# The third group of dilated query and key tiles as four plain tiles, with fewer weight sums and another pace for the rest

## The chip, the core and the metric

The kernel runs on one core of one Trainium2 chip. The metric is the device time of one execution in microseconds, the median over runs. The core has a matrix engine (TensorE, PE in the profile, with its weight loads as PEld), VectorE (DVE), ScalarE (ACT) and GpSimd (POOL); SyncE (SP) issues most of the loads, POOL issues other DMAs, and 16 DMA engines move the data of both queues.

## The reference

One decoder layer over x of 512 tokens x 1024 channels, in float32. A single projection of x gives queries, keys and values of three causal token mixers and three gates:

```python
proj = x @ w_in
(da_q, da_k, da_v, sb_q, sb_k, sb_v, dl_q, dl_k, dl_v, gates) = jnp.split(proj, _split_points(), axis=-1)
...
merged = (g[:, :, 0] * (o_da @ w_branch_da) + g[:, :, 1] * (o_sb @ w_branch_sb)
          + g[:, :, 2] * (o_dl @ w_branch_dil))
return merged @ w_out
```

`da` is differential attention (4 heads), `sb` stick-breaking attention (8 heads), `dl` dilated attention: three window groups of 4 heads of 128 channels, so `dl_q` and `dl_k` have 12 column tiles of 128 each. Output head `hd` of the dilated mixer needs the tiles `4 * g + hd` of the three groups g. After the mixer come a layer norm, a squared-ReLU MLP with 4096 hidden channels, a gated per-layer embedding and a second layer norm:

```python
x = layer_norm(DEEPNORM_ALPHA * x + m, ln1_g[i], ln1_b[i])
hid = jax.nn.relu(x @ w_up[i])
c = jnp.square(hid) @ w_down[i]
ple = jax.nn.sigmoid(x @ w_ple_gate[i]) * (p[i] @ w_ple[i])
x = layer_norm(DEEPNORM_ALPHA * x + c + ple, ln2_g[i], ln2_b[i])
```

## The kernel before

**Precision.** Every large product is done with both operands split into a high and a low part, as three matmuls: high x high, high x low, low x high (`mm3`, L86 to L89). Weights come from DRAM in chunks of 128 x 1024 (512 KB) into a ring of six raw buffers; ACT casts a chunk to its high part (L262), DVE subtracts to get the low part (L264), into a ring of five pairs. `pump` and `split_next` run these splits ahead of TensorE. SP issues the loads (`fill`, L194 to L219) in the order of the chunks, one queue in order: a load that must wait for its data or for a free buffer holds up all loads behind it.

**Items.** The work of TensorE is a list of items in a fixed order (`main_order`, L36 to L53, then the gates, branches, output projection, embedding and MLP). The loop at L2177 walks through it. Around each item it calls `step()`, which lets the attention heads that are in flight (Python generators: `sb_head`, `da_block`, `dil_head`) emit their next piece; an item whose `mm` is a generator with one `yield` gets a second `step()` in its middle. So attention is woven between the projection's matmuls.

**A plain tile** ("T", `t_item`, L311) is one item: one weight chunk, eight k blocks, three matmuls of 512 columns each, 24 in all, and its result is put away by one operation over 512 columns (L343 on ACT for `dl_q`, L346 on DVE for `dl_k`).

**A group** ("G", `group_items`, L354) computes four tiles, that is two query-key pairs, with seven products in place of eight: weights and x are cut into 2 x 2 blocks, and sums of weight blocks meet sums of x blocks. Each product is taken for both pairs over half of the tokens (256 columns): 7 x 2 x 4 x 3 = 168 matmuls, in seven items. It uses seven weight chunks, three from the weights themselves and four that are sums of weight blocks (`qsum`), and puts its results away in halves (L394, L396, L398, L407, L440 and L441). There are three groups, each of which holds two query-key pairs of the dilated heads 2 and 3. Groups 0 and 1 lie behind the value tiles; group 2 lies between the second and the third differential query-key pair, and dilated head 3 needs it.

**Weight sums.** The same scheme of seven products serves values, gates, branches and the MLP. All their weight sums are made in DRAM by DMAs that POOL issues (`sum_steps`, L1212): a plain copy of a 512 KB block to a scratch tensor or an accumulating copy onto it. A sum of the kind `up_steps` takes eight steps, of the kind `two_steps` four, of `down_steps` eight; the queue of them is in the order of use (values, `qsum`, gates `msum` and branches `bsum`, `gsum`, then the MLP's `usum` and `dsum`), with four sums in progress at a time, and two towards its end. Each step of a sum waits on POOL's queue until the step before it in that sum has landed. The loads of `usum` and `dsum` chunks by SP wait for the sum in turn. POOL's queue also carries the dilated heads' value stores and loads (`keep` L520, `values_of` L528) and the accumulations straight into a raw buffer (`then_add`, L176).

**Pace.** When a step is emitted is set by credits (L2222 to L2228): each item adds its `size` times its `rate`, and each whole credit emits one step. Items without a rate of their own get 2.8, 2.3 or 3.3 by their place in the list (L960); those with 3.3 are the differential query and key tiles. Group items have 0.6 (L382), output projection items 1.4 (L1055), of which those before `wout_at + 6` count. From the last of the embedding's items on, each item adds 0.78 (L2225). There are 208 steps in all. On POOL each step also waits for a mark, a recent operation of DVE, so that steps do not run far ahead of the stream.

Of the kernel before, what the change touches and what calls it, by code (L numbers as in the profile page):

```python
# [10 lines left out]
F32 = mybir.dt.float32  # L11
# [7 lines left out]
P = 128  # L19
# [16 lines left out]
def main_order():  # L36


    o = [("T", "sb_q", 0), ("T", "sb_k", 0), ("T", "sb_q", 1), ("T", "sb_k", 1), ("V", "sb_v", 0)]
    for j in (2, 3):  # L40
        o += [("T", "sb_q", j), ("T", "sb_k", j)]
    for h in range(2):
        for g in range(3):
            o += [("T", "dl_q", 4 * g + h), ("T", "dl_k", 4 * g + h)]
    o += [("V", "dl_v", 0), ("V", "da_v", 0), ("V", "dl_v", 1), ("V", "dl_v", 2)]
    pairs = [(("dl_q", 4 * g + h), ("dl_k", 4 * g + h)) for h in (2, 3) for g in range(3)]
    groups = [("G", tuple(pairs[2 * i:2 * i + 2]), i) for i in range(3)]
    o += groups[:2]
    for d in range(4):
        if d == 2:  # L50
            o += groups[2:]
        o += [("T", "da_q", d), ("T", "da_k", d)]
    return o  # L53


def trunk(tc, a, out):
    nc = tc.nc
    es = ExitStack()
    with es:
# [4 lines left out]
        dram = es.enter_context(tc.tile_pool(name="dram", bufs=1, space=bass.MemoryType.DRAM))  # L64
# [9 lines left out]
        def slot(name, dt=F32):  # L74
            return big.tile([P, 512], dt, name=nm(name), tag="s", bufs=NSLOT)

        def small(name, n):
            return one.tile([P, n], F32, name=nm(name), tag=f"sm{n}", bufs=12 if n < 8 else 8)
# [89 lines left out]
        def chunk(src, w):  # L168
            return chunk_of(load(src, w))
# [114 lines left out]
        items = []  # L284
# [21 lines left out]
        T = {}  # L306
# [42 lines left out]

        HB = slice(0, 256)  # L350
        HC = slice(256, 512)
        qsum = [[dram.tile([P, 1024], F32, name=f"qsum{m}_{i}") for i in range(4)] for m in range(3)]

        def group_items(gi, pairs):  # L354

# [601 lines left out]
            item([], mm, ev, size=0.08)  # L957

        for j, it in enumerate(items):
            it.setdefault("rate", 2.8 if j < 12 else 2.3 if j < 52 else 3.3)  # L960

        gate_alone(0, 1)
        gate_alone(1, 2)
# [64 lines left out]
        def wout_items():  # L1028
            for half in range(2):
                cs = [chunk(a["wo"][half, c].rearrange("p k n -> p (k n)"), 1024) for c in range(4)]  # L1030
                for tt in range(4):
                    ks = (4, 5, 6, 7, 0, 1, 2, 3) if tt == 2 and not half else range(8)

                    def mm(ps, tt=tt, cs=cs, ks=ks):
                        for k in ks:
                            c = cs[k // 2]
                            s = slice((k % 2) * 512, (k % 2) * 512 + 512)
                            h, lo = merged_T[k // 4, tt // 2, k % 4 // 2]
                            q = slice(k % 2 * 256 + tt % 2 * P, k % 2 * 256 + tt % 2 * P + P)
                            nc.tensor.matmul(ps, h[:, q], c["h"][:, s], start=k == ks[0], stop=False)  # L1040
                            nc.tensor.matmul(ps, h[:, q], c["l"][:, s], start=False, stop=False)
                            nc.tensor.matmul(ps, lo[:, q], c["h"][:, s], start=False, stop=k == ks[-1])  # L1042

                    def ev(ps, tt=tt, half=half):
                        y = xn.pop((tt, half))
                        if not half:
                            x1sum[tt] = small("lsm", 2)
                        i = nc.vector.scalar_tensor_tensor(y, y, ALPHA, ps, op0=OP.mult, op1=OP.add,
                                                           accum_out=x1sum[tt][:, half:half + 1])
                        st["added"] = getattr(i, "ins", i)  # L1050
                        x1[tt, half] = y
                        if half:
                            pending.append(ln1_gen(tt))
                    item(cs if tt == 3 else [], mm, ev, need=cs, bank=at_bank)
                    items[-1]["rate"] = 1.4  # L1055
                    for t in {0: [(1, 1, 0), (1, 1, 1)], 1: [(0, 1, 0), (0, 1, 1)]}.get(tt, ()) if not half else ():
                        turn_item(*t)

# [153 lines left out]
        def sum_steps():  # L1212
            def up_steps(sums, w, flat=False):
                w = [w[i] if flat else w[i].rearrange("p k n -> p (k n)") for i in range(4)]
                a1, a2, a3, a4 = sums
                yield a1, w[2], False
                yield a3, w[0], False
                yield a1, w[3], True
                yield a3, w[2], True
                yield a2, a1, False  # L1220
                yield a2, w[0], True
                yield a4, a2, False
                yield a4, w[1], True

            def two_steps(sums, w, flat=False):
                w = [w[i] if flat else w[i].rearrange("p k n -> p (k n)") for i in range(4)]
                a1, a2 = sums
                yield a1, w[2], False
                yield a1, w[3], True
                yield a2, a1, False  # L1230
                yield a2, w[0], True

            def down_steps(m):
                w = [a["wd"][m, i].rearrange("p k n -> p (k n)") for i in range(4)]
                b1, b2, b3, b4 = dsum[m]
                yield b1, w[0], False
                yield b3, w[1], False
                yield b1, w[1], True
                yield b3, w[3], True
                yield b2, b1, False  # L1240
                yield b2, w[3], True
                yield b4, b2, False
                yield b4, w[2], True

            def issue(o, i, plus):
                if plus:
                    i = nc.gpsimd.dma_start(o, i, accum_op=OP.add, max_dma_last_dim=4096)  # L1247
                else:
                    i = nc.gpsimd.dma_start(o, i, max_dma_last_dim=4096)

                tc.add_manual_dep(getattr(i, "ins", i), marks[0].name, mybir.DependencyInfo(
                    mybir.DependencyClass.Sync, mybir.DependencyReason.DATA), reason="spread over the main stream")

            w = a["wv"].rearrange("g c p k n -> g c p (k n)")
            todo = deque(two_steps(vsum[n][m], [w[1 + 2 * n + i // 2, i % 2 * 2 + m] for i in range(4)], True)
                         for n in range(2) for m in range(2))
            todo.extend(up_steps(qsum[m], a["wq"][m]) for m in range(3))
            for n in range(3):
                todo.extend(two_steps(msum[n][m], a["wgm"][n, m]) for m in range(2))
                if n:  # L1260
                    todo.append(up_steps(bsum[2 * (n == 1)], a["wbq"][int(n == 1)]))
            todo.extend(two_steps(gsum[m], a["wg"][m]) for m in range(2))
            for kind, m in ("u0", "u1", "d0", "u2", "u3", "d1", "d2", "u4", "u5", "d3", "d4", "u6", "u7", "d5", "d6"):
                m = int(m)
                todo.append(up_steps(usum[m], a["wu"][m]) if kind == "u" else down_steps(m))
            run = []
            while todo or run:
                while todo and len(run) < (4 if len(todo) > 9 else 2):
                    run.append(todo.popleft())
                for g in list(run):  # L1270
                    s = next(g, None)
                    if s is None:
                        run.remove(g)
                    else:
                        issue(*s)
                        yield
# [338 lines left out]
        wout_at = len(items)  # L1615
# [362 lines left out]
        def dil_head(hd):  # L1978
# [35 lines left out]
            for c in range(4):  # L2014
                s = slice(c * P, c * P + P)
                for g in range(2):
                    o = L12[c // 2][:, (c % 2) * 256 + g * P:(c % 2) * 256 + g * P + P]
# [6 lines left out]
            for c in range(4):  # L2024
                o = L12[c // 2][:, (c % 2) * 256:(c % 2) * 256 + 256]
# [34 lines left out]
            with tc.high_priority():  # L2060
# [3 lines left out]
                for c in range(4):  # L2064
                    o = L12[c // 2][:, (c % 2) * 256:(c % 2) * 256 + 256]
# [5 lines left out]
            if hd == 0:  # L2071
                yield
                values = values_of(hd)
            for _ in range({0: 6, 1: 2, 3: 1}.get(hd, 0)):
                yield

            src0 = {}
# [4 lines left out]
            for half in range(2):  # L2082
# [4 lines left out]
                t = slot("pt0")  # L2087
# [5 lines left out]
            for g in range(2):  # L2093
# [4 lines left out]
                t = slot("pt12")  # L2098
# [5 lines left out]
            for kb in range(4):  # L2104
                n = 256 if kb < 3 else P
# [67 lines left out]
        credit = 0.0  # L2173
# [3 lines left out]
        for n, it in enumerate(items):  # L2177
# [20 lines left out]
            if prev is not None:  # L2198
                prev[0]["ev"](prev[1])
                todo, lead = prev[0].get("then", ((), 0))  # L2200
# [18 lines left out]
            if n == 13:  # L2219
                pending.append(tables())  # L2220

            if 5 <= n < wout_at + 6:  # L2222
                credit += it["size"] * it.get("rate", 1.0)
            elif n > ple_at + 6:
                credit += 0.78  # L2225
            while credit >= 1:
                credit -= 1
                next(sum_steps_, None)  # L2228
# [148 lines left out]
```

## Time and profile before

| | us |
|---|---|
| median of 3 runs | 1032.52 |
| lowest and highest run | 1031.86, 1037.55 |
| the profiled execution | 1029.26 |
| its span, first to last instruction | 1027.5 |

A line of the profile's table of groups names the source line, the engine, the operation, what it writes and reads, the shape, the count, then the busy time, the mean duration of one in ns, and the idle time before it with what ended it. A timeline line gives start, duration, engine, line, operation, tiles, shape and count, and in brackets the idle time before it and what released it. Matmuls are pipelined: a matmul's own duration is longer than the distance to the next one's start, and the distance is what a matmul costs. TensorE's granted clock was 0.999 of full speed in the profiled execution.

### The profile page before, as it was taken

To read this page: it belongs to the slowest core of one execution; us is meant where nothing else is said; L and a number is where in the kernel's file an instruction comes from. 1 tells how busy PE (TensorE), PEld (TensorE's weight loads), DVE (VectorE), ACT (ScalarE), POOL (GpSimd) and SP (SyncE) were. 2 spreads that over 40 slices of the span, in tenths; PEclk is the share of its full clock that TensorE was granted. 3 is DMA by queue.
4 is the path that set the end of the run, shared out by engine and by line. 5 is a ranking of instruction groups with operands and counts; after the bars stand their busy time and mean duration, and the time that the engine had idled before them with its cause. 6 is when DMAs were issued, how large, how long until landed. Compare 5 with 4: busy or idle time off the path is not lost.

```text
span 1027.5 us, 15644 instructions
## 1 busy us (share of the span) xinstructions
PE 1014.6 (99%) x5626; PEld 879.0 (86%) x5626; DVE 794.4 (77%) x1411; ACT 614.7 (60%) x1055; POOL 208.8 (20%) x311
## 2 busy tenths in 40 slices
PE   9999999999999999999999999999999999999997
PEld 6888887888998898888888888889999999999786
DVE  6888697788657776886788885897778778768785
ACT  7566566775544656566655733866666656556551
POOL 0232320121412123111121130222121211111101
PEclk9999999999999999999999999999999999999999
DMA  8999993888999999879999893799999999998932
GB/s 312 286 306 288 259 271 96 209 206 259 288 319 283 253 287 276 220 201 263 352 291 273 294 323 109 182 248 355 338 323 332 318 324 350 327 332 263 297 148 82
DMA packets 79885, 275.99 MB, mean 269 GB/s; under 512 B 9816, under 2 KB 10600, under 8 KB 79808
## 3 DMA queue, kind: packets, MB, share of 16 engines
q0 software_dynamic: 37712, 135.08, 52.4%
q1 hardware_dynamic: 41520, 138.99, 36.6%
q8 instruction: 44, 0.72, 0.3%
q10 hardware_dynamic: 576, 0.92, 0.2%
q14 instruction: 33, 0.27, 0.1%
HBM read 267.59 MB, written 116.42 MB: 374 GB/s over the span
## 4 chain that ended last, share of the span: by engine, by line
PE 92%; DVE 4%; DMA 1%; ACT 1%; issue 1%; DVEq 0%; SPq 0%; ACTq 0%
PE mm L87 9%; PE mm L88 9%; PE mm L89 9%; PE at L1431 4%; PE at L1430 4%; PE at L1432 4%; PE at L752 2%; PE at L751 2%; PE at L750 2%; PE mm L750 2%; PE mm L751 2%; PE mm L752 2%; PE at L89 2%; PE at L88 2%; PE at L87 2%; PE at L1042 1%
## 5 line engine op out<-in xcount | busy, mean ns | idle before, releaser
L264 DVE TENSOR_TENSOR wl<-raw,wh 128x1024 fp32r<-128x1024 f32 (+1 forms) x274 | 330.2, 1214 | 111.4 <-ACT wh L262 110.2
L262 ACT CAST wh<-raw 128x1024 fp32r<-128x1024 f32 (+1 forms) x274 | 283.7, 1042 | 206.9 <-PE mm L88 104.3
L87 PE MATMUL mm<-xhT,wh 128*128 128x512 f32 (+1 forms) x254 | 95.5, 376 | 1.1 <-DVE dl_k L346 1.1
L89 PE MATMUL mm<-xhT,wl 128*128 128x512 f32 (+1 forms) x254 | 94.4, 371 | 0.0
L88 PE MATMUL mm<-xlT,wh 128*128 128x512 f32 (+1 forms) x254 | 94.1, 370 | 0.0
L1431 PE MATMUL at<-wl,hh 128*128 128x512 f32 x188 | 73.8, 393 | 1.0 <-DVE wl L264 1.0
L1430 PE MATMUL at<-wh,hh 128*128 128x512 f32 x188 | 73.9, 393 | 0.5 <-ACT hid L1402 0.5
L1432 PE MATMUL at<-wh,hl 128*128 128x512 f32 x188 | 73.2, 389 | 0.0
L87 PE MATMUL mm<-x1hT,wh 128*128 128x256 f32 x256 | 72.8, 284 | 0.0
L88 PE MATMUL mm<-x1lT,wh 128*128 128x256 f32 x256 | 72.4, 283 | 0.0
L89 PE MATMUL mm<-x1hT,wl 128*128 128x256 f32 x256 | 72.4, 283 | 0.0
L87 PEld LDWEIGHTS mm<-xhT,wh 128*128 128x128 f32 x254 | 47.9, 189 | 8.9 <-issue 1.2
L89 PEld LDWEIGHTS mm<-xhT,wl 128*128 128x128 f32 x254 | 47.8, 188 | 8.3
L88 PEld LDWEIGHTS mm<-xlT,wh 128*128 128x128 f32 x254 | 47.9, 189 | 7.5
L1247 POOL DMA_DIRECT2D usum<-in_wu_dram x32 | 27.0, 843 | 134.5 <-DVE wl L264 61.5
L87 PEld LDWEIGHTS mm<-x1hT,wh 128*128 128x128 f32 x256 | 48.9, 191 | 1.9
L88 PEld LDWEIGHTS mm<-x1lT,wh 128*128 128x128 f32 x256 | 48.9, 191 | 1.5
L89 PEld LDWEIGHTS mm<-x1hT,wl 128*128 128x128 f32 x256 | 48.9, 191 | 0.0
L1247 POOL DMA_DIRECT2D dsum<-in_wd_dram x28 | 24.1, 860 | 106.4 <-DVE wl L264 30.1
L1432 PEld LDWEIGHTS at<-wh,hl 128*128 128x128 f32 x188 | 35.3, 188 | 7.6
L1430 PEld LDWEIGHTS at<-wh,hh 128*128 128x128 f32 x188 | 35.5, 189 | 7.1 <-ACT hid L1402 0.7
L1431 PEld LDWEIGHTS at<-wl,hh 128*128 128x128 f32 x188 | 35.5, 189 | 7.0 <-DVE wl L264 1.3
(676 smaller groups left out, 2857.3 us busy)
## 6 DMA issues: line engine op xcount, KB each, us to landing
usum<-in_wu_dram POOLq DMA_DIRECT2D x48, 512.0 KB, 8.9
dsum<-in_wd_dram POOLq DMA_DIRECT2D x42, 512.0 KB, 8.9
raw<-usum SPq DMA_DIRECT2D x32, 512.0 KB, 8.5
raw<-dsum SPq DMA_DIRECT2D x28, 512.0 KB, 7.8
raw<-in_wt_dram SPq DMA_DIRECT2D x26, 512.0 KB, 7.8
raw<-in_wd_dram SPq DMA_DIRECT2D x25, 512.0 KB, 9.7
raw<-in_wu_dram SPq DMA_DIRECT2D x24, 512.0 KB, 8.3
qsum<-in_wq_dram POOLq DMA_DIRECT2D x18, 512.0 KB, 8.9
```

The lines of the kernel that those rows point to most:

```text
L87: nc.tensor.matmul(ps, wh, xh, start=start, stop=False, skip_group_check=True)
L88: nc.tensor.matmul(ps, wh, xl, start=False, stop=False, skip_group_check=True)
L89: nc.tensor.matmul(ps, wl, xh, start=False, stop=stop, skip_group_check=True)
L262: i = nc.scalar.copy(h, raw)
L264: i = nc.vector.tensor_sub(lo, raw, h.bitcast(F32))
L750: nc.tensor.matmul(ps, h[:, q], c["h"][:, n], start=go, stop=False, skip_group_check=True)
L751: nc.tensor.matmul(ps, h[:, q], c["l"][:, n], start=False, stop=False, skip_group_check=True)
L752: nc.tensor.matmul(ps, lo[:, q], c["h"][:, n], start=False, stop=end, skip_group_check=True)
L1247: i = nc.gpsimd.dma_start(o, i, accum_op=OP.add, max_dma_last_dim=4096)
L1430: nc.tensor.matmul(ps, h[:, q], c["h"][:, s], start=go, stop=False, skip_group_check=True)
L1431: nc.tensor.matmul(ps, h[:, q], c["l"][:, s], start=False, stop=False, skip_group_check=True)
L1432: nc.tensor.matmul(ps, lo[:, q], c["h"][:, s], start=False, stop=end, skip_group_check=True)
```

## The change

Group 2 becomes four plain tiles at the same place, `dl_q` and `dl_k` of its two query-key pairs. Its weight sums (`qsum[2]`, eight steps) are no longer made, so 200 steps are left, and the weights of the group are laid out as plain tiles by the host's `_layout`, which follows `main_order`. The four new tiles take the default rate of their place in the list. That rate goes from 3.3 to 3.0, the output projection's from 1.4 to 2.4 with one item fewer counted, and the MLP's from 0.78 to 0.66. Dilated head 3 waits for one more call of its generator before its weights are transposed (L2074).

```diff
     pairs = [(("dl_q", 4 * g + h), ("dl_k", 4 * g + h)) for h in (2, 3) for g in range(3)]
-    groups = [("G", tuple(pairs[2 * i:2 * i + 2]), i) for i in range(3)]
-    o += groups[:2]
+    o += [("G", tuple(pairs[2 * i:2 * i + 2]), i) for i in range(2)]
     for d in range(4):
         if d == 2:
-            o += groups[2:]
+            o += [("T", *t) for p in pairs[4:] for t in p]
         o += [("T", "da_q", d), ("T", "da_k", d)]
...
-        qsum = [[dram.tile([P, 1024], F32, name=f"qsum{m}_{i}") for i in range(4)] for m in range(3)]
+        qsum = [[dram.tile([P, 1024], F32, name=f"qsum{m}_{i}") for i in range(4)] for m in range(2)]
...
-            it.setdefault("rate", 2.8 if j < 12 else 2.3 if j < 52 else 3.3)
+            it.setdefault("rate", 2.8 if j < 12 else 2.3 if j < 52 else 3.0)
...
-                    items[-1]["rate"] = 1.4
+                    items[-1]["rate"] = 2.4
...
-            todo.extend(up_steps(qsum[m], a["wq"][m]) for m in range(3))
+            todo.extend(up_steps(qsum[m], a["wq"][m]) for m in range(2))
...
-            for _ in range({0: 6, 1: 2, 3: 1}.get(hd, 0)):
+            for _ in range({0: 6, 1: 2, 3: 2}.get(hd, 0)):
                 yield
...
-            if 5 <= n < wout_at + 6:
+            if 5 <= n < wout_at + 5:
                 credit += it["size"] * it.get("rate", 1.0)
             elif n > ple_at + 6:
-                credit += 0.78
+                credit += 0.66
```

## The prediction

> **What bounds the kernel now.** I read the page first, then TensorE's timeline for the pace of its matmuls, then the waits of the DMA queues, and last the timeline of POOL, which issues the sum steps.
>
> ```profile
> span 1027.5 us, 15644 instructions
> PE 1014.6 (99%) x5626; PEld 879.0 (86%) x5626; DVE 794.4 (77%) x1411; ACT 614.7 (60%) x1055; POOL 208.8 (20%) x311
> DMA  8999993888999999879999893799999999998932
> q0 software_dynamic: 37712, 135.08, 52.4%
> q1 hardware_dynamic: 41520, 138.99, 36.6%
> PE 92%; DVE 4%; DMA 1%; ACT 1%; issue 1%; DVEq 0%; SPq 0%; ACTq 0%
> ```
>
> TensorE is busy in 99% of the span and carries 92% of the chain that ended last. A busy PE is not a PE at its peak, but here it hardly ever waits, so a change in its matmuls shows one for one, and all that any other engine can give back is in its few idle moments. The second full resource is the DMA: 9 tenths or more in most slices, with the dip to 3 in slice 25 (about 617 to 642 us, the output projection). The POOL queue (q0) costs 0.524 x 1027.5 / 135.08 = 3.99 us of all 16 engines per MB, so 2.1 us for a sum step of 0.524 MB; a load of SP's (q1) costs 0.366 x 1027.5 / 138.99 x 0.524 = 1.4 us.
>
> The idle moments, in TensorE's timeline:
>
> ```profile
> 357.56 0.71 PE L1944 MATMUL at<-dl_v,wT 128*128 128x128 f32 x4 [0.68 <-ACT scr L1949]
> 972.17 0.47 PE L1430 MATMUL at<-wh,hh 128*128 128x512 f32 x1 [0.54 <-ACT hid L1402]
> 975.12 0.50 PE L1431 MATMUL at<-wl,hh 128*128 128x512 f32 x1 [1.01 <-DVE wl L264]
> ```
>
> The first lies inside the third tile group, the other two in the last stage of the MLP. They are 2.23 us together.
>
> **Part 1: four plain tiles for the group, on TensorE.** A group is 7 products x 2 pairs x 4 k x 3 = 168 matmuls of 256 columns; four plain tiles are 4 x 8 x 3 = 96 of 512 columns. The price of each is the distance of its starts. First a product of the group (24 matmuls and the first one behind them), then a plain tile of the same stretch:
>
> ```profile
> 364.84 0.28 PE L87 MATMUL mm<-u5h,wh 128*128 128x256 f32 x1
> ...
> 367.60 0.28 PE L89 MATMUL mm<-u5h,wl 128*128 128x256 f32 x1
> 367.72 1.06 PE L1944 MATMUL at<-dl_v,wT 128*128 128x128 f32 x8
> ```
> ```profile
> 339.62 0.40 PE L87 MATMUL mm<-xhT,wh 128*128 128x512 f32 x1
> ...
> 344.87 0.39 PE L89 MATMUL mm<-xhT,wl 128*128 128x512 f32 x1
> 345.09 0.33 PE L146 MATMUL at<-da_ka,da_qa 128*128 128x384 f32 x1
> ```
>
> (367.72 - 364.84) / 24 = 0.120 us, and (345.09 - 339.62) / 24 = 0.228 us. So the group costs 168 x 0.120 = 20.2 us, the tiles 96 x 0.228 = 21.9 us: **+1.7 us**, all of it on the path. That is far less than the 8/7 in arithmetic, since a short matmul costs more per column.
>
> The Trainium skill's page "TensorE: Matmul & The Clock Gate", section "Back-to-back issue gap", gives a warm gap of N / 2.4 + 2.5 ns, which is 109 and 216 ns here. By that this part would cost 2.4 us, so the rule speaks against the change a little more than the rows do; the rows stand 11 to 12 ns above it at both widths.
>
> **Part 2: what the group no longer asks of DVE, ACT and the queues.**
>
> ```profile
> L264 DVE TENSOR_TENSOR wl<-raw,wh 128x1024 fp32r<-128x1024 f32 x6 | 7.3, 1222 | 1.9 <-ACT wh L262 1.7
> L262 ACT CAST wh<-raw 128x1024 fp32r<-128x1024 f32 x5 | 5.2, 1043 | 1.5 <-PE mm L88 1.5
> ...
> L396 DVE TENSOR_TENSOR dl_k<-mm,gs 128x256 f32<-128x256 f32 x3 | 1.8, 612 | 0.0
> ```
> ```profile
> L346 DVE COPY dl_k<-mm x6: 683/684/692, 98.8 to 171.2; 128x512 f32<-128x512 f32 x6
> ```
>
> The group splits 7 weight chunks and puts its results away in halves: DVE 7 x 1.22 + 6 x 0.61 = 12.2 us. The tiles split 4 and put away whole: DVE 4 x 1.22 + 2 x 0.68 = 6.2 us. ACT loses three casts of 1.04 and the half copies. Neither engine is on the path, except at 357.56, where attention's operations on ACT and DVE queued among these splits and TensorE waited 0.68 us. With half the work there I count that wait as gone: **-0.7 us** (between 0, if another attention step is late there, and -0.7). The four tiles call the attention generators 8 times where the group's seven items called them 7 times, and the extra wait in the last dilated head takes that call back, so attention sits where it sat. SP loads 4 chunks instead of 7 and none that waits for a sum.
>
> **Part 3: eight sum steps fewer, and earlier ones.** The eight steps of the third group's sums are gone: 8 x 2.1 + 3 x 1.4 = 21 us of DMA time. That is hidden under TensorE, and worth what it does for waits. Here the issue schedule decides, and I worked it out from the credits in the code. Before, 138 of 208 steps have been emitted when the first MLP item begins, and the 208th falls at the second `part_b` of tile 6. These are those two items on TensorE, the 139th, the 206th and the 208th step on POOL, and what SP meets in between:
>
> ```profile
> 700.08 0.28 PE L87 MATMUL mm<-x1hT,wh 128*128 128x256 f32 x1
> ...
> 912.50 0.28 PE L87 MATMUL at<-t7h,wh 128*128 128x256 f32 x1
> ```
> ```profile
> 698.76 0.81 POOL L1249 DMA_DIRECT2D usum<-in_wu_dram  x1
> ...
> 950.39 0.81 POOL L1247 DMA_DIRECT2D dsum<-in_wd_dram  x1 [3.52 <-DVE wl L264]
> ...
> 963.64 0.81 POOL L1247 DMA_DIRECT2D dsum<-in_wd_dram  x1 [5.31 <-DMA dsum<-dsum]
> ```
> ```profile
> SPq L213 <- DMA dsum<-in_wd_dram: 20.4, 2, 11.5
> ```
> ```profile
> 935.95 21.93 SPq L213 DMA_DIRECT2D raw<-dsum  x4
> ```
> ```profile
> 947.84 5.94 DMA raw<-dsum
> ...
> 957.97 5.58 DMA raw<-usum
> ```
>
> The stream asks for a step every (912.50 - 700.08) / 69 = 3.1 us, POOL delivers one every (963.64 - 698.76) / 69 = 3.8 us, since each step of a chain waits for the one before it to land. So POOL begins level with TensorE and ends 51 us behind, and the last sums come too late: SP stands 20.4 us in two waits for them, every load behind it in its queue waits too, and the chain of waits goes through those loads (947.84, 957.97) into the 0.54 and 1.01 us of idle TensorE.
>
> After: the third group's steps are missing at the head of the queue, and 36 instead of 30 steps fall into the differential tiles and the four new ones. At the first MLP item 144 of 200 are emitted, 56 are left instead of 70, at 0.66 per item. Even at POOL's present 3.84 us they end at about 703 + 55 x 3.84 = 914, and the third from last, which SP waits for until about 957 today, is issued at 906 and has landed by 914. It would have to take 4.5 us per step to be late. So SP's two waits go, and with them the idle rows at 972 and 975: **-1.5 us** (between 0, if the buffers run dry there for another reason, and -2). What is late next in that stage is nothing that I see: TensorE has no idle row elsewhere in the MLP.
>
> **Part 4: the queue that gets fuller.** 36 steps and 12 loads are 36 x 2.1 + 12 x 1.4 = 92 us of DMA time in a stretch of about 88 us, where 30 and 15 were 84 in 87. Behind them on POOL lie the accumulations for the first gate (L176) and the value loads of the last dilated head (L528), for which TensorE waits at L2106.
>
> ```profile
> 309.36 2.56 POOL L1247 DMA_DIRECT2D msum<-in_wgm_dram  x3 [7.63 <-DVE wl L264]
> ...
> 332.04 0.84 POOL L1247 DMA_DIRECT2D msum<-in_wgm_dram  x1 [12.92 <-DVE L L2066]
> ...
> 345.93 0.81 POOL L1249 DMA_DIRECT2D bsum<-in_wbq_dram  x1
> ...
> 388.51 1.72 POOL L176 DMA_DIRECT2D raw<-in_wgm_dram  x1
> ...
> 401.74 0.79 POOL L528 DMA_DIRECT2D dl_vh<-values  x1
> 402.75 1.51 POOL L528 DMA_DIRECT2D dl_vh<-values  x2 [0.21 <-PE at L1930]
> ```
> ```profile
> 405.27 0.48 PE L750 MATMUL mm<-wh,xhT 128*128 128x512 f32 x1
> ...
> 420.31 1.68 PE L2106 MATMUL at<-pt,dl_vh 128*128 128x256 f32 x8
> ```
> ```profile
> dl_vh<-values POOLq DMA_DIRECT2D x12, 256.0 KB, 7.8
> ```
>
> POOL stands here for DVE's progress (12.92 us before 332.04), not only for landings, and when let go it issued 7 steps from 332.04 to 345.93, 2.3 us each, with four chains open. The value loads stand behind 36 steps that begin at 309.36. At 2.3 to 2.6 us (the lower by those rows, the upper by the 92 us of DMA time) they are issued by 392 to 403, or later only because the stream itself is not there yet, as now at 401.74. They land 1.5 + 7.8 us later, by 412, and TensorE wants them at 420.31 + 1.0 for parts 1 and 2 + one generator step of about 2.7, so at 424. L176 has more room: its product begins after four gate items of 12 x 0.228 us, not before 416, and it was issued at 388.51. I cost this part at nothing; if the cover is gone, each us of POOL beyond about 10 costs a us. The two output-projection tiles that now ask for 2.4 steps each put 5 steps instead of 3 into the dip of the DMA row, and the layer norm's operations on POOL come four or more tiles (22 us) later.
>
> **Sum.** +1.7 - 0.7 - 1.5 = -0.5 us on the profiled execution's 1029.26 us (span 1027.5 and 1.8 around it). That execution lies 3.3 us below the median of 1032.52, so I put the sum on the median: **1032.0 us**.
>
> **Rivals.** *A, the fuller queue decides (slower).* If POOL needs over (424 - 9.3 - 309.4) / 36 = 2.9 us per step between the groups and the gates, TensorE waits at L2106. For it: DMA at 0.9 or more in these slices, and the 3.8 us of the MLP. Against: in the MLP two chains are open, here four, and the rows give 2.3. Halfway between 2.9 and 3.6, at 3.25, the loads land at 309.4 + 36 x 3.25 + 9.3 = 435.7, 12 us late: 1044 us.
>
> *B, the weight loads set TensorE's pace (faster).* 72 loads go.
>
> ```profile
> 364.73 0.19 PEld L87 LDWEIGHTS mm<-u5h,wh 128*128 128x128 f32 x1
> 364.84 0.19 PEld L88 LDWEIGHTS mm<-u5l,wh 128*128 128x128 f32 x1
> ```
>
> At 0.19 us each that would be 13.7 us less instead of 1.7 more, with the waits gone 1032.5 - 13.7 - 2.2 = 1017 us. Against: the next load starts 0.11 us after the last, so loads overlap, and the matmuls keep the pace of their columns. The Trainium skill's "Perfetto Trace Analysis", "Identifying the Most-Contended Engine", would judge headroom by the share of weight loads, 86% here, rather than by matmul time; by that rule this rival would be the one.
>
> *C, the last sums are not what TensorE waits for.* Then 972 and 975 stay, +1.7 - 0.7 = +1.0: 1033.5. For it: the stage also splits hidden activations on ACT and DVE, and both idle rows name those. Against: 20.4 us of SP's queue just ahead.
>
> *D, the relief is wider.* TensorE is not busy for 1027.5 - 1014.6 = 12.9 us, of which I have counted 2.2. If fewer splits and earlier sums take away a quarter of the rest, the gain is 2.7 us more: 1029.3. For it: DVE at 77% and DMA at 9 tenths, both relieved. Against: the rest is in pieces too small to be named.
>
> **How the numbers follow.** Forecast 0.55, C 0.17, D 0.15, A 0.10, B 0.03. A measurement of this kernel can tell about 0.5% (5 us) from no change. Forecast, C and D lie inside that, and B outside. D reaches over it with 0.05, A lies over it. So faster 0.08, same 0.82, slower 0.10. The three runs before spread from 1031.86 to 1037.55; the range takes in D below and the small end of A and that spread above: 1027.5 to 1037.5.
>
> **What would show it.** Right: no idle row of TensorE at 970 to 976; SP without a wait for `dsum`; the last `dsum` step on POOL near 914 instead of 963.64; plain tiles at 0.228 us per matmul; `L528` issued by about 405. Wrong: an idle row before L2106 or before the first gate's third product names A; a stretch of four tiles much under 21.9 us names B; idle rows left near 972 with POOL early name C.

## The result and the profile after

The kernel after takes 1031.55 us in the median of 20 runs (1029.37 to 1036.71), the kernel before, timed beside it on the same chip, 1036.64 us in 20 runs (1031.86 to 1040.25). The ratio is 0.9959, with a 95% interval of 0.9946 to 0.9972: some 4.2 us less in the mean (1036.51 to 1032.26); the medians lie 5.1 us apart. The predicted 1032.0 us is half a microsecond off. The predicted gain, 0.5 us, is far too small: the forecast stood on a median of three runs, 1032.52, which is low for the kernel before. One run of experiment 5 (3610 us) and one of experiment 10 (1690 us) lie far above all others of their kernels; they are counted in the runs and medians below, not in the ratios.

The two profiled executions tell the opposite of the medians. Before was profiled at 1029.26 us, below every one of its 20 runs; after at 1034.05 us, above its median. So the traces can't be subtracted from each other as they are; they have to be read stage by stage. In after's source, lines behind L50 have a number lower by one than in before's. First the page of after:

```profile
span 1032.3 us, 15466 instructions
...
PE 1018.5 (99%) x5554; PEld 878.4 (85%) x5554; DVE 791.5 (77%) x1404; ACT 610.5 (59%) x1046; POOL 202.3 (20%) x303
...
DMA  8999993688899999979999995689999999988522
...
q0 software_dynamic: 36560, 130.89, 50.6%
q1 hardware_dynamic: 41088, 137.42, 36.5%
...
PE 85%; issue 6%; DVE 4%; DMA 3%; ACT 2%; POOL 1%; DVEq 0%; ACTq 0%; POOLq 0%
```

72 matmuls and 4.2 MB on POOL's queue are gone, as the change says. But the chain that ended last holds only 85% of TensorE, where it was 92%, with 6% of issue and 3% of DMA: something new makes TensorE wait. It is in TensorE's timeline, at the first gate's third product:

```profile
418.82 1.03 PE L2095 MATMUL at<-ident,L 128*128 128x128 f32 x8
421.90 0.50 PE L749 MATMUL at<-wh,xhT 128*128 128x512 f32 x1 [2.05 <-DVE on L1964]
...
422.71 0.62 PE L749 MATMUL at<-wh,xhT 128*128 128x512 f32 x1
423.12 0.63 PE L750 MATMUL at<-wl,xhT 128*128 128x512 f32 x1
...
426.11 0.42 PE L751 MATMUL at<-wh,xlT 128*128 128x512 f32 x1
```

It is idle for 2.05 us, and then, from the fourth on, its matmuls start 0.43 us apart for 3.4 us (422.71 to 426.11) where 0.228 is usual. The chain of waits names what came late, and POOL's timeline when that was issued:

```profile
397.22 19.62 DMA raw<-in_wgm_dram
...
418.46 0.96 ACT wh L261
...
419.44 1.23 DVE wl L263
```
```profile
389.85 1.03 POOL L175 DMA_DIRECT2D raw<-in_wgm_dram  x1
...
397.22 0.90 POOL L175 DMA_DIRECT2D raw<-in_wgm_dram  x1 [1.39 <-DVE da_kla L137]
...
403.36 0.81 POOL L527 DMA_DIRECT2D dl_vh<-values  x1 [2.91 <-PE at L1929]
...
408.62 0.75 POOL L527 DMA_DIRECT2D dl_vh<-values  x1 [1.66 <-DMA raw<-in_wgm_dram]
...
925.04 0.80 POOL L1246 DMA_DIRECT2D dsum<-in_wd_dram  x1 [4.12 <-PE at L1431]
```

The second accumulation for that gate (L176 of before, L175 now) is issued at 397.22, where the two of before were out at 388.51, and takes 19.6 us to land, where it took 15.1 in before (and 14.4 in experiment 1, the kernel before again). So its data is there 13.2 us later, 8.7 by the issue and 4.5 by the landing. The last line is the good half: the last `dsum` step leaves at 925.04 and not at 963.64, and SP has no wait for `dsum` any more. The windows view shows both ends; its columns are the stretch, then the busy time of PE, PEld, DVE, ACT and POOL (with counts), the granted clock, the DMA share and GB/s. Before, then after:

```profile
390.00:420.00 30.00, 29.59 (x158) 24.67 (x157) 24.53 (x87) 19.48 (x50) 6.50 (x11) 1.00 0.89 256
420.00:450.00 30.00, 30.00 (x159) 25.51 (x158) 23.87 (x58) 16.18 (x36) 5.50 (x7) 1.00 0.85 226
...
950.00:975.00 25.00, 23.57 (x125) 19.88 (x123) 19.31 (x28) 13.54 (x20) 4.38 (x7) 1.00 0.91 290
```
```profile
390.00:420.00 30.00, 29.86 (x160) 25.24 (x158) 23.63 (x83) 19.49 (x50) 8.24 (x11) 1.00 1.05 263
420.00:450.00 30.00, 28.09 (x137) 23.85 (x138) 22.05 (x57) 15.46 (x32) 4.03 (x6) 0.94 0.74 212
...
950.00:975.00 25.00, 25.00 (x147) 22.13 (x146) 23.81 (x35) 17.04 (x26) 0.00 (x0) 1.00 0.59 187
```

Ahead of the gate the DMA share goes from 0.89 to 1.05, that is full; in the slice behind it TensorE loses 2.05 us of idleness and 0.06 of the clock over 30 us, 1.8 us. At the end TensorE no longer waits. The two lines that answer to Parts 1 and 2 are a plain tile, (346.38 - 340.91) / 24 = 0.228 us per matmul, and the wait inside the stretch, 0.51 us where it was 0.68:

```profile
340.91 0.40 PE L86 MATMUL mm<-xhT,wh 128*128 128x512 f32 x1
...
346.38 0.33 PE L145 MATMUL at<-da_ka,da_qa 128*128 128x384 f32 x1
...
358.47 0.71 PE L1943 MATMUL at<-dl_v,wT 128*128 128x128 f32 x4 [0.51 <-ACT scr L1948]
```

### The profile page after: what moved, and what is told of

Same layout as the page of the kernel before. It is cut to its first block, busy times and chain, and to the rows that moved or that the text cites. A ratio compares the mean times of both kernels' runs of the same rounds, so it can differ in the third digit from the quotient of the medians.

```text
span 1032.3 us, 15466 instructions
## 1 busy us (share of the span) xinstructions
PE 1018.5 (99%) x5554; PEld 878.4 (85%) x5554; DVE 791.5 (77%) x1404; ACT 610.5 (59%) x1046; POOL 202.3 (20%) x303
## 4 chain that ended last, share of the span: by engine, by line
PE 85%; issue 6%; DVE 4%; DMA 3%; ACT 2%; POOL 1%; DVEq 0%; ACTq 0%; POOLq 0%
PE mm L86 8%; PE mm L88 8%; PE mm L87 8%; PE at L1429 4%; PE at L1430 4%; PE at L1431 4%; PE at L749 2%; PE at L750 2%; PE at L751 2%; DMA raw<-in_wgm_dram 2%; PE at L88 2%; PE at L87 2%; PE at L86 2%; PE mm L749 1%; PE at L1041 1%
## 5 line engine op out<-in xcount | busy, mean ns | idle before, releaser
L263 DVE TENSOR_TENSOR wl<-raw,wh 128x1024 fp32r<-128x1024 f32 (+1 forms) x271 | 326.7, 1214 | 109.8 <-ACT wh L261 108.1
L86 PE MATMUL mm<-xhT,wh 128*128 128x512 f32 (+1 forms) x270 | 103.9, 385 | 1.1 <-DVE dl_k L345 1.1
L88 PE MATMUL mm<-xhT,wl 128*128 128x512 f32 (+1 forms) x270 | 102.4, 379 | 0.0
L87 PE MATMUL mm<-xlT,wh 128*128 128x512 f32 (+1 forms) x270 | 102.1, 378 | 0.0
L86 PEld LDWEIGHTS mm<-xhT,wh 128*128 128x128 f32 x270 | 50.9, 188 | 10.1 <-issue 1.2
L88 PEld LDWEIGHTS mm<-xhT,wl 128*128 128x128 f32 x270 | 50.8, 188 | 9.6
L87 PEld LDWEIGHTS mm<-xlT,wh 128*128 128x128 f32 x270 | 50.9, 188 | 8.6
```

The source lines that it names most:

```text
L86: nc.tensor.matmul(ps, wh, xh, start=start, stop=False, skip_group_check=True)
L87: nc.tensor.matmul(ps, wh, xl, start=False, stop=False, skip_group_check=True)
L88: nc.tensor.matmul(ps, wl, xh, start=False, stop=stop, skip_group_check=True)
L263: i = nc.vector.tensor_sub(lo, raw, h.bitcast(F32))
```

## The experiments

The theory after the result: the gain is at the end of the MLP, where the usual execution of before loses far more than the one profiled; the tiles themselves cost time; and fuller POOL and DMA queues take some of the gain back at the first gate. The rivals: the tiles are what gains (less DVE and DMA work), or the rates of the sum steps do nothing. Each kernel was timed in five rounds beside the kernel before, in three batches.

To compare profiled executions, I cut the span in three at two starts on TensorE that exist in all of them: the last product of the second group (its first matmul is the only one of 0.38 to 0.39 us there) and the first matmul behind the first layer norm. In before, and in the cleanest kernel with tiles (the eighth experiment):

```profile
308.40 0.38 PE L87 MATMUL mm<-u5h,wh 128*128 128x256 f32 x1
...
661.84 0.50 PE L1169 MATMUL at<-wh,x1hT 128*128 128x512 f32 x1
```
```profile
308.82 0.38 PE L86 MATMUL mm<-u5h,wh 128*128 128x256 f32 x1
...
663.52 0.50 PE L1168 MATMUL at<-wh,x1hT 128*128 128x512 f32 x1
```

| profiled execution (us) | up to the first | between | from the second to the end of the span |
|---|---|---|---|
| before, the profile of the prediction | 308.4 | 353.4 | 365.7 |
| before, again (1) | 308.7 | 353.6 | 372.8 |
| after | 309.7 | 358.0 | 364.6 |
| after, again (4) | 308.5 | 358.7 | 364.7 |
| tiles, old rates (2) | 309.4 | 367.1 | 364.7 |
| tiles, rate 2.4 (5) | 308.6 | 354.7 | 365.1 |
| tiles, sums late (7) | 309.7 | 354.8 | 365.8 |
| tiles, rates 2.4 and 1.2 (8; again: 11) | 308.8; 309.9 | 354.7; 354.7 | 364.7; 364.7 |
| groups, rates 1.2 and 2.4 (9) | 308.3 | 355.6 | 365.0 |
| groups, rates 1.2 and 3.2 (10) | 308.8 | 354.8 | 363.5 |
| groups, sums early (3) | 308.4 | 358.3 | 365.4 |
| groups, rates 1.3 and 2.4 (6) | 309.1 | 356.7 | 365.8 |

The middle stretch can be cut once more, at the first `at<-wh,o4h` matmul of the branches. Up to there all six executions with the group took 226.1 to 226.2 us, whatever their pace, and the four with tiles and rate 2.4 or 2.0 (5, 7, 8, 11) took 227.3 to 227.4: the tiles cost 1.2 us. Behind it the kernel before took 127.4 us, those four 127.3 to 127.4, and experiments 9, 10 and 6 129.5, 128.6 and 130.6.

**1. The kernel before, again** (no edit).

> The kernel before once more, for a second profile of it beside its many runs. The profile on which the prediction rests shows 1.55 us of idle TensorE at 972 to 975. Late sums (the theory of the prediction, with its size open): a usual execution of this kernel has SP waiting for dsum at 935 to 960, and more than 1.55 us of idle TensorE behind it, 3 to 8 us with the slower matmuls that follow an idle stretch. Rival (the stretch of the third group has the larger loss): idle TensorE at 970 to 980 stays near 1.5 us, and the loss between 330 and 430 is larger than in the first profile. Time against itself: ratio 1.000.

1037.0 us (1031.21 to 1038.27, 12 runs), ratio 0.9996 (0.9976 to 1.0017). Its profiled execution took 1036.84 us, about the median, and it is not the one that the prediction was built on. The queue's wait, the sums on POOL, TensorE and the window:

```profile
SPq L213 <- DMA dsum<-in_wd_dram: 27.3, 2, 18.4
```
```profile
957.85 0.81 POOL L1247 DMA_DIRECT2D dsum<-in_wd_dram  x1 [4.14 <-issue]
...
971.26 0.81 POOL L1247 DMA_DIRECT2D dsum<-in_wd_dram  x1 [5.34 <-DMA dsum<-dsum]
```
```profile
962.54 0.79 PE L1430 MATMUL at<-wh,hh 128*128 128x512 f32 x1 [4.23 <-ACT wh L262]
963.79 0.79 PE L1431 MATMUL at<-wl,hh 128*128 128x512 f32 x1 [0.47 <-DVE wl L264]
964.39 0.63 PE L1432 MATMUL at<-wh,hl 128*128 128x512 f32 x1
964.81 0.63 PE L1430 MATMUL at<-wh,hh 128*128 128x512 f32 x1
...
982.70 0.50 PE L1431 MATMUL at<-wl,hh 128*128 128x512 f32 x1 [1.01 <-DVE wl L264]
```
```profile
950.00:975.00 25.00, 20.30 (x89) 16.32 (x88) 12.25 (x17) 9.17 (x14) 4.91 (x8) 0.86 0.84 251
```

The last step leaves 8 us later than in the first profile, SP's longer wait is 18.4 and not 11.5 us, and TensorE is idle for 4.23 + 0.47 + 1.01 = 5.7 us. The two are one chain: ACT's cast ahead of the 4.23 us, at 961.44, had stood 11.10 us for a load `raw<-dsum`. In the window it also loses 0.14 of the clock over 25 us, 3.5 us: some 9 us in all, where the first profile showed 1.55. The third stretch is 8.2 us longer than after's.

**2. The tiles with the old rates.**

```diff
-            it.setdefault("rate", 2.8 if j < 12 else 2.3 if j < 52 else 3.0)
+            it.setdefault("rate", 2.8 if j < 12 else 2.3 if j < 52 else 3.3)
...
-                    items[-1]["rate"] = 2.4
+                    items[-1]["rate"] = 1.4
...
-            for _ in range({0: 6, 1: 2, 3: 2}.get(hd, 0)):
+            for _ in range({0: 6, 1: 2, 3: 1}.get(hd, 0)):
...
-            if 5 <= n < wout_at + 5:
+            if 5 <= n < wout_at + 6:
...
-                credit += 0.66
+                credit += 0.78
```

> The plain tiles and the 200 steps with the old rates (3.3, 1.4, 0.78, and one call less in dilated head 3). 39 steps fall between the groups and the gates, 36 in the changed kernel and 30 before; at the MLP 52 are left. Late sums: the last sum is issued by about 905, no wait of SP for dsum, and the whole gain of the change is there: ratio 0.994 to 0.997. The fuller queue (rival A): the accumulation for the first gate lands later than in the changed kernel, TensorE idles 3 to 6 us before the gate's third product, and the time is 2 to 6 us above the changed kernel's.

1042.63 us (1040.86 to 1042.88, 6 runs), ratio 1.0059 (1.0039 to 1.0079): slower than before. 39 steps now fall between the groups and the gates. TensorE and the chain:

```profile
427.88 2.47 PE L2105 MATMUL at<-pt,dl_vh 128*128 128x256 f32 x5 [7.34 <-DMA dl_vh<-values]
```
```profile
409.56 1.09 POOL raw L175
410.66 17.08 DMA dl_vh<-values
...
427.88 2.47 PE at L2105 x5
```

This is the prediction's rival A in full, at its own place: the value loads are issued at 410.66, land 17.1 us later, and TensorE stands for 7.34 us; the clock in the slice from 420 to 450 is 0.83. The end has no wait for `dsum`. So the tiles alone do not gain with the old pace. Two things were taken back here at once, the three steps and the call in dilated head 3 that lets the values be asked for later (TensorE was ready for them 111.1 us after the first mark, in experiment 5 at 113.9); how the 7.34 us divide between them was not tried.

**3. The groups kept, the sums earlier.** The kernel before with more steps in the output projection, and steps again from the first of the embedding's items on.

```diff
-                    items[-1]["rate"] = 1.4
+                    items[-1]["rate"] = 2.4
...
-            elif n > ple_at + 6:
+            elif n >= ple_at:
```

> All three groups and all 208 steps, but the steps come earlier: output projection rate 2.4 instead of 1.4, and the steps of 0.78 begin with the first embedding item instead of the eighth; 62 steps are left at the MLP instead of 69. Late sums: the last sum is issued near 938 instead of 964, SP's waits for dsum shrink to under 5 us, TensorE's idle time at 970 to 976 goes, and the time falls by the gain of the change plus the 1.7 us of the tiles: ratio 0.993 to 0.996. Rival (the gain comes from the stretch of the tiles): ratio 0.998 to 1.000.

1033.93 us (1033.24 to 1034.88, 12 runs), ratio 0.998 (0.9967 to 0.9993). The end stall is gone without any tile (SP's one wait for `dsum` is 5.6 us), but most of the gain is given back in the layer norm, whose small POOL operations queue behind the steps that were put there. On POOL a `dsum` step stood 6.46 us for the landing before it, and the layer norm's L1003 came behind it at 662.15, where it was at 657.36 in before:

```profile
663.66 1.75 PE L1078 MATMUL at<-ident,xn 128*128 128x128 f32 x8 [2.59 <-DVE xn L1013]
666.64 0.80 PE L1169 MATMUL at<-wh,x1hT 128*128 128x512 f32 x1 [1.24 <-ACT x1r L1091]
```

The ratio is the one that the rival had, but not for the rival's reason.

**4. The kernel after, again** (no edit).

> The changed kernel once more, for a second profile. Its first profile shows 2.05 us of idle TensorE at 421.9, behind an accumulation for the first gate that took 19.6 us to land, and ten matmuls of 0.43 us behind it. If this belongs to the kernel (the fuller queue), it is there again, 1 to 4 us in all; if it was chance, not. No wait of SP for dsum and no idle TensorE at 950 to 980 in either case. Ratio 0.996.

1032.88 us (1029.76 to 1036.45, 12 runs), ratio 0.9968 (0.995 to 0.9986). The gate stall is there again, 2.73 us idle at 421.40, behind an accumulation that was issued at 396.98 and took 19.4 us. So it is not a chance of one execution. Both profiled executions lie above their median, though, and 11 of the 20 runs of after took under 1031.7 us; whether the stall is in those too, no profile shows.

**5. After, with fewer steps in the tiles**: 28 instead of 36 between the groups and the gates.

```diff
-            it.setdefault("rate", 2.8 if j < 12 else 2.3 if j < 52 else 3.0)
+            it.setdefault("rate", 2.8 if j < 12 else 2.3 if j < 52 else 2.4)
```

> The changed kernel with the rate 2.4 instead of 3.0 in the differential and the four new tiles: 28 steps between groups and gates instead of 36, 63 left at the MLP instead of 56. The fuller queue (the loss at 421 comes from the 36 steps): the accumulation for the first gate lands in about 10 us, the idle 2 to 3 us and the slow matmuls behind it go, the last sum is issued near 942, still early enough for SP, and the time falls by 3 us against the changed kernel: ratio 0.992 to 0.995. Rival (the four tiles themselves leave attention or the gate short, whatever the steps): the idle stretch before the gate's third product stays, ratio 0.996.

1030.3 us (from 1029.83, 10 runs), ratio 0.9955 (0.994 to 0.9971). POOL, TensorE and the window:

```profile
386.96 0.88 POOL L175 DMA_DIRECT2D raw<-in_wgm_dram  x1 [1.72 <-DVE wl L263]
```
```profile
419.17 0.50 PE L749 MATMUL at<-wh,xhT 128*128 128x512 f32 x1 [0.28 <-DVE on L1964]
```
```profile
390.00:420.00 30.00, 29.72 (x160) 25.15 (x159) 25.13 (x87) 20.23 (x51) 2.75 (x4) 1.00 0.57 176
```

The accumulation is out 10.3 us earlier and lands in 10.1 us, the DMA share ahead of the gate falls from 1.05 to 0.57, and the stall shrinks to 0.28. The stretch is 3.3 us shorter than in after: that is what the fuller queue costs in a profiled execution with the stall. In the ratio that gain doesn't show: 0.9955 stands against 0.9959 and 0.9968 for after, where I expected 0.992 to 0.995. Seven steps more are left for the MLP, and SP waits 4.9 us for one, without effect on TensorE.

**6. The groups kept, with more steps in the gates** (first edit) and in the output projection.

```diff
-                    items[-1]["rate"] = 1.0
+                    items[-1]["rate"] = 1.3
...
-                    items[-1]["rate"] = 1.4
+                    items[-1]["rate"] = 2.4
```

> All three groups and all 208 steps; gate items rate 1.3 instead of 1.0 and output projection 2.4 instead of 1.4, so that 61 steps are left at the MLP instead of 69, without the steps among the embedding items that stalled the layer norm in the run before. Late sums: the last sum is issued near 934, SP's waits for dsum go, and with them the 9 us that the second profile of the kernel before loses from 950 to 1000; no tiles to pay for: ratio 0.989 to 0.993, faster than the changed kernel. Rival (groups need the tiles' relief, or steps in the gate stage stall the gates as the steps before it did): loss in the gate stage of 3 us or more, ratio 0.995 to 0.998.

1029.19 us (1027.8 to 1033.28, 12 runs), ratio 0.9952 (0.9935 to 0.997). I expected 0.989 to 0.993. The profiled run is its slowest and shows no stall at the end, but small ones in the branches and the first MLP items. They stand behind loads of sum chunks that were slow to land, 13.81 us for `raw<-bsum` at 573.77 and 13.61 for `raw<-usum` at 695.57; the median for `raw<-bsum` was 7.4 in before:

```profile
593.55 0.33 PE L950 MATMUL mm<-ident,graw 128*128 128x128 f32 x1 [1.28 <-DVE graw L932]
...
710.64 0.39 PE L87 MATMUL mm<-x1hT,wh 128*128 128x256 f32 x1 [1.66 <-ACT up L1358]
```

So the whole gain of the change can be had with the group kept, by pace alone.

**7. The tiles with late sums**: after, with the old rates behind the tiles and a low one in them, so that 68 steps are left for the MLP, as in before (70).

```diff
-            it.setdefault("rate", 2.8 if j < 12 else 2.3 if j < 52 else 3.0)
+            it.setdefault("rate", 2.8 if j < 12 else 2.3 if j < 52 else 2.0)
...
-                    items[-1]["rate"] = 2.4
+                    items[-1]["rate"] = 1.4
...
-            if 5 <= n < wout_at + 5:
+            if 5 <= n < wout_at + 6:
...
-                credit += 0.66
+                credit += 0.78
```

> The four plain tiles, but with sums as late as before: rate 2.0 in the tiles, output projection 1.4 and MLP 0.78 as before, so 24 steps between groups and gates and 68 left at the MLP (69 before). Late sums: SP waits for dsum again, TensorE loses 5 to 10 us from 950 to 1000, and with the 1.7 us that the tiles cost the time is that of the kernel before or a little above: ratio 0.998 to 1.003. Rival (the tiles bring the gain themselves): ratio 0.995 to 0.997.

1031.88 us (1030.23 to 1034.58, 12 runs), ratio 0.9977 (0.9961 to 0.9993): a gain, though a smaller one, where I expected none. What brings it is open. SP's wait and TensorE:

```profile
SPq L212 <- DMA dsum<-in_wd_dram: 18.5, 2, 11.6
```
```profile
976.76 0.50 PE L1430 MATMUL at<-wl,hh 128*128 128x512 f32 x1 [0.59 <-DVE wl L263]
```

Here SP stands 18.5 us, and it costs TensorE 0.59 us. With the first profile (20.4 us, the longest 11.5: 1.55 us idle) and experiment 1 (27.3 us, the longest 18.4: 5.7 us idle and the clock), the price does not grow in step with the wait: the loads that are ahead cover a wait of some 11 us. Of the 6.9 us beyond it in experiment 1, 4.2 came as idleness, and 3.5 more by the clock. These are three executions; the rule is my reading of them.

**8. After, with more steps in the gates** (first edit) **and fewer in the tiles.**

```diff
-                    items[-1]["rate"] = 1.0
+                    items[-1]["rate"] = 1.2
...
-            it.setdefault("rate", 2.8 if j < 12 else 2.3 if j < 52 else 3.0)
+            it.setdefault("rate", 2.8 if j < 12 else 2.3 if j < 52 else 2.4)
```

> The run with rate 2.4 in the tiles, and gate items at 1.2: 59 steps left at the MLP, the last sum near 927. If the end was already early enough with 63 left, the same time as that run within 1 us; if 63 were a little late, up to 3 us below it. Against the run with groups and gate rate 1.3 it should stand 1.7 us above, the price of the tiles on TensorE: ratio 0.991 to 0.995.

1030.29 us (1029.37 to 1031.17, 9 runs), ratio 0.996 (0.9946 to 0.9975). SP has no wait for `dsum`, the gate stall is 0.28, the end has none. It is level with experiment 5, in a narrow spread; I expected 0.991 to 0.995.

**9 and 10. The groups kept, at the same gentler pace**, the better version that the table pointed to, at 63 and 61 steps left for the MLP. Experiment 10 has 3.2 where the last line of the diff has 2.4. The first of the two edits is that of the gate items, the second that of the output projection.

```diff
-                    items[-1]["rate"] = 1.0
+                    items[-1]["rate"] = 1.2
...
-                    items[-1]["rate"] = 1.4
+                    items[-1]["rate"] = 2.4
```

> The third group stays a group with its own sums. Gate items give 1.2 instead of 1.0 steps, output projection items 2.4 instead of 1.4, the rest as before. Theory (the gain is the end stall, the tiles are a price of 1.7 us): 63 steps left at the first MLP item, the last dsum step on POOL near 950, no idle row of TensorE over 1 us at 950 to 980 and none over 1 us in the gates; 1028 to 1029 us, ratio 0.991 to 0.995, and 1.5 to 2.5 us below the tile version of the same call. Rival (the tiles themselves are worth time, by less DVE and DMA work): level with the tile version or above it.

> As the kernel above, with 3.2 steps per output projection item: 61 left at the first MLP item, last dsum step near 940. If the buffers cover some 12 us of late sums, as the theory has it, this is the same time as the kernel above within 1 us. If the layer norm's POOL operations are held up by the extra steps, TensorE has an idle row over 1 us at 655 to 675 and the time is 1 to 4 us longer.

1030.49 us (1029.16 to 1031.22, 9 runs), ratio 0.9947 (0.993 to 0.9964), and 1030.3 us (from 1028.82, 10 runs), ratio 0.9948 (0.993 to 0.9966). Both are the same time, as the theory had it for 10, though 10 has the layer norm's wait of 1.17 us that its expectation named for a loss; experiment 9 is 1.5 to 2.5 us above what I expected. The last `dsum` steps leave at 954.55 and 954.51, SP waits 3.5 and 5.3 us, and TensorE does not wait at the end. In experiment 9 it waits elsewhere, in the branches, where loads `raw<-bsum` took a median of 13.0 us to land, and in the first MLP items:

```profile
591.70 0.33 PE L950 MATMUL mm<-ident,graw 128*128 128x128 f32 x1 [0.82 <-DVE graw L932]
...
705.54 0.39 PE L87 MATMUL mm<-x1hT,wh 128*128 128x256 f32 x1 [0.46 <-ACT up L1358]
707.69 0.39 PE L87 MATMUL mm<-x1hT,wh 128*128 128x256 f32 x1 [0.45 <-ACT up L1358]
```

**11. Experiment 8 again**, on the chip of 9 and 10.

> The kernel after with 2.4 instead of 3.0 steps in the differential and the four new tiles and 1.2 instead of 1.0 in the gate items, once more, to stand on the same chip as the two group kernels. Theory: 1029.5 to 1031, ratio 0.994 to 0.997, 1.5 to 2.5 us above the first kernel of this call. Rival (tiles worth time): below it or level.

1030.4 us (1029.45 to 1030.89, 9 runs), ratio 0.9948 (0.9931 to 0.9965): level with both group kernels, where I had expected the group kernels 1.5 to 2.5 us below it. That was a miss, and level is what the rival had: tiles worth time. The tiles do cost 1.2 us up to the branches. But behind that point experiments 9 and 10 pay 1.2 to 2.1 us for their raised rates, and the tile kernel at the same two rates pays nothing. I take that for the eight more sum steps and three more chunks that have to get through the same queues; no run tests it. As a whole the exchange of group for tiles is worth nothing that could be measured here; the pace is worth 5 us. No version beats the others of these clearly, nor after: this kernel gave 0.996 in experiment 8 and 0.9948 now, which is as much as parts them from after's 0.9959 and 0.9968.

One miss runs through all the expectations: the last `dsum` step left POOL 5 to 22 us later than they put it, in each experiment for which they named a time.

## Why the prediction was right in the number and wrong in the sum

**Part 1 held.** Plain tiles run at 0.228 us per matmul in after too, as in before, 12 ns above the gap that the section "Back-to-back issue gap" in the Trainium skill's page "TensorE: Matmul & The Clock Gate" gives for an isolated matmul. Parts 1 and 2 made +1.0 us; up to the branches it is +1.2.

**Part 2 failed in its place.** The wait at 357.56 was put down to the group's splits and counted as gone. It is 0.51 us in after, with 6.2 us of DVE work in place of 12.2: the splits were hardly its cause. Of the 0.7 us, 0.2 came.

**Part 3 had the right mechanism and the wrong size, and it is the term that carries the result.** "SP's two waits go, and with them the idle rows at 972 and 975" is what happened; the last step left at 925 for 914, still early enough. But "-1.5 us (between 0 ... and -2)" took its size from one execution that was the luckiest of all: 20.4 us of waits, just beyond what the loaded buffers cover. In a usual execution (experiment 1, at the median) the longer wait is 7 us longer, beyond the cover, and the end costs 9 us. The spread of the three runs, from 1031.86 to 1037.55, was the sign: the profiled execution lay below all of them, and the one part of the kernel known to be late was the one to suspect. The 8 us don't arise at the end: POOL's steps in experiment 1 run within 0.7 us of the first profile up to 756 us, are 4.9 us behind it at 776.80, where a step stood 5.60 us for the landing before it (2.20 in the first profile), and drift to 7 us by 938. Why landings are slower in one execution than in another of the same program, no run shows.

**Part 4, "I cost this part at nothing", failed.** It counted the landing of the accumulations as usual: "L176 has more room: its product begins ... not before 416, and it was issued at 388.51". With 36 steps it was issued at 397.22 and landed in 19.6 us; it took 15.1 in before already, and 10.1 and 8.2 in experiments 5 and 8, where fewer steps lie ahead of it. So the margin was counted in time of issue alone, while the landing grows with the same load. The 92 us of DMA time in 88 us of stream, worked out in that very part, was the warning; and the list of idle rows left out one of 0.41 us at 414.17, just ahead of that gate's product. The value loads were out at 403.36 to 408.62, past the 405 that was named, and TensorE did not wait for them. Price: 3.3 us between the marks in the profiled executions (after against experiment 5 or 8).

**The rivals.** A was real, at a fraction: at the first gate in after, as the last part of the prediction named it, and at L2106 itself with three steps more and one call less (experiment 2). C fell: with the sums early, no wait is left at the end, whatever ACT and DVE split there. B fell: with 72 weight loads fewer, the matmuls of plain tiles kept their 0.228 us. D's small pieces did not show: TensorE's time not busy is 13.8 us in after, 12.9 before.

**The sum, as the profiled executions show it**, from experiment 1 to after and after again: -8.2 from the second mark to the end, +1.2 for the tiles, +3.3 to 4.0 at the gate, together -3 to -3.7 us; measured 4.2 less in the mean, with an interval of 2.9 to 5.6. The gate stands in it at its full price, and both profiled executions of after are slow ones among its runs. That 1032.0 met 1031.55 is luck, two errors that cancel: a base that was 4 us low and a gain that was 4 us small.

## What to carry to other kernels

A wait that buffers just cover in the profiled execution is not priced by its idle row there: ask how much of the queue's wait is left uncovered if it grows by a few microseconds, and look whether the profiled run lies at the edge of the timed ones. Where a queue gets fuller, price issue and landing together: here the same 512 KB accumulation landed in 10.1 us with a DMA share of 0.57 ahead of the gate, in 15.1 with 0.89 and in 19.6 with 1.05. And when a change comes in one piece with new pacing, try the pacing alone; here it gave the whole gain.

## What the runs showed of the hardware

**An idle stretch is paid twice.** After 2.05 us of idleness (after), 2.73 us (after again) and 4.23 us (experiment 1) TensorE's matmuls start 0.43 us apart, half the usual pace: for 3.4 us from 422.71 and from 422.22 in the first two, from 962.54 to 968.65 in the third; after 1.01 us (before at 975.12), 1.17 us (experiment 10) and 1.66 us (experiment 6) they do not. The mean clock follows: 0.993 to 0.996 in the profiled executions with such a stall, 0.997 to 0.999 in those without. The Trainium skill's page "TensorE: Matmul & The Clock Gate", section "What's actually happening", has a clock at half speed after at least one idle window of about 3.4 us, in windows that run freely. The 3.4 us of slow matmuls in after agree with such a window; the idleness here was shorter than one, and the measurement decides: 2.05 us were enough, in one execution. Ahead of it lay 1.03 us of transposes with the identity (418.82); should they count as idle, it was 3.1 us, still shorter than the window.

**The end of the span.** From the last store's issue on ACT's queue (1024.07 of a span of 1027.5 in before, 1028.02 of 1032.3 in after) to the end it is 3.4 to 3.5 us in all six executions with the group that were looked at and 4.3 to 4.5 in all seven with the tiles. That 0.9 us lies behind the last store in a part of the program that the change doesn't touch. It comes on top of the 1.2 us in the price of the tiles, and is in the last column of the table; its cause was not tried and stays open.
